# Gating of a conv MLP kept inside its up projection, with h tiles that take over the activations' memory kind by kind

## The chip, the cores and the metric

The kernel runs on one core of a Trainium2 chip. The metric is the time of one execution in microseconds (us). The engines are PE (TensorE, matrix products), DVE (VectorE), ACT (ScalarE), POOL (GpSimd) and SP (SyncE, which here only issues transfers).

## The reference

One layer on 656 columns (a prompt of 512 tokens with 16 meta tokens ahead, and 8 streams of 16). Its first half ends in an output projection (called "out" below) that is added to x. The change touches the second half:

```
up = rmsnorm(x) @ w_up              # 2048 -> 2 * 5632
g, v = up[..., :D_FF], up[..., D_FF:]
gext = concatenate([hist, g])       # two earlier rows of g
gc = conv_b + sum_k gext[k:k+seqlen] * conv_w[k]     # k = 0, 1, 2
h = gelu(gc) * v
y = x + h @ w_down                  # 5632 -> 2048, then a last rmsnorm
```

## The kernel before

Activations lie transposed: 128 channels on the partitions, 640 columns. The 5632 channels of g, v and h are 44 tiles, f = 0 to 43.

**Products.** Each fp32 operand is split into a high part (a cast by ACT) and a low part (a subtraction by DVE); a product is three matmuls, wh·xh, wh·xl and wl·xh. One helper issues all ACT, DVE and POOL operations, so the profile shows them under L130, and all matmuls stand under L157: operations are told apart by their tile names.

**Order.** The program is emitted once, with a modelled clock. Background work (evictions, splits, gating) are Python generators that `E.spawn` puts into a list and `E.tick` (L231) steps between matmuls. An engine runs its own instructions strictly in the order of emission and waits on semaphores, so a spawned step has a fixed place in each engine's queue.

**Weights.** `load_raw` (transfer at L197) loads four weight tiles at a time into one of four buffers `wraw`; ACT casts them to `wh` (four buffers), DVE subtracts to `wl`, and then the next load is issued. `wtile` (L250) runs the six matmuls of a weight tile; one such load thus feeds 24 matmuls.

**Out projection** (tiles n = 0 to 15, L1326 to L1352). Each n is evicted by `evict_x2` (L1232): DVE adds PSUM to x, the sum is stored as x3, squared by ACT and added to `ssq` by DVE. `mix` (L1207) then forms from two n's, pair j, the seven kinds of activations (B11, T1, B21, B22, T2, T3, T4) of a one-level Strassen scheme, and `split_mix` (L1223) writes their high and low parts: pairs 0 to 5 into `XT`, pairs 6 and 7 into `XH`, which is a view of `H[0]`, the operand of out, and so has to wait for out's last matmuls.

**Up projection** (L1461 on). For each f seven chains, one per kind, in two halves of K: 14 units of 12 matmuls, 168 per f. `Up` loads and combines weights. `evict_up` (L1432) makes g and v of f. For f < `NEARLY` = 11, `early` (L1418) runs `gate` (L1388: scale by rstd, conv, gelu, times v) and stores h to DRAM (`h_d`). For the other 33, `late` (L1424) stores g and v to DRAM (`g_d`, `v_d`).

**Down projection** (L1565). h of f is the operand k = f, kept as `hid` (high and low) in a ring of 21 places. The places and the accumulators `acc` lie over `XT` and `XH`, all in one pool that is opened after up. `load_h` (L1490) brings back the 11 stored h, `split_h` (L1518) splits them, then the 16 tiles x3 are loaded into `acc` (L1532), and `gates` (L1539) loads g and v of f = 11 to 43, gates and splits them during the down projection. The work runs in chunks of K, `DCH` = 11, 10, 10 and 9 k's by 16 n's; a chunk's places come free together when it ends:

```
for f in range(NEARLY, NFF):
    while f - RING > passed[0]:
        yield
```

The last four k's form a tail in two column halves, at the end of which y is normalised and stored.

Of the kernel before, what the change touches and what calls it, by code (L numbers as in the profile page):

```python
# [4 lines left out]
F32 = mybir.dt.float32  # L5
# [12 lines left out]
NEARLY = len(DCH[0])  # L18
RING = 21
# [255 lines left out]
def body(tc, A):  # L275
# [20 lines left out]
    H = [hp0.tile([128, 8, 2, NT], F32R, name="H0"), hp1.tile([128, 8, 2, NT], F32R, name="H1")]  # L296
# [20 lines left out]
    with tc.manual_schedule():  # L317
# [861 lines left out]
        cm_x, xp = E.open("x", waits="tile")  # L1179
# [75 lines left out]
        class Up:  # L1255
            def load(self, f, name, half):
                tag = "wraw" if (name == "A22") == (f > 0) and name != "A12" else "wr"
                self.put(f, name, half, tag)
                SP.dma_start(out=R[f, name, half], in_=A["wup"][(f * 4 + UP_LOADS.index(name)) * 2 + half])
# [8 lines left out]
            def start(self):  # L1268
                for name in ("A11", "A21"):
                    for half in range(2):  # L1270
                        self.load(0, name, half)

            def add(self, u):
# [5 lines left out]
                if p == "P1":  # L1279
                    self.put(f, "P1", h, "wraw" if f else "wr")  # L1280
# [45 lines left out]
        up = Up()  # L1326
        pss = [mm4() for _ in range(2)]
# [9 lines left out]
        for n in range(2, 16):  # L1337
            ps, t = mm4()
            for k in range(8):
                xh, xl = hsl(0, k, NC)  # L1340
                if n == 15 and k == 2:
                    up.start()
                if n == 15 and k in (4, 6):
                    up.split(k // 2 - 2)
# [5 lines left out]
            E.spawn(evict_x2(n, ps, t), 0, True)  # L1350
        while any(e in E.bg for e in E.bg):
# [12 lines left out]
        rps = [bank1(), bank1()]  # L1364
        rg = rstd_calc(ssq, rstd, 2 * XW, rps)
        next(rg)
        cm_f6.__exit__(None, None, None)
        cm_f7, f7 = E.open("f7", side="right", waits="tile")
        up.pool = f7
        for name in ("A22", "A12"):  # L1370
            for half in range(2):
                up.load(0, name, half)
            if name == "A22":
                up.add(2)
                up.add(3)

# [47 lines left out]
        def late(f, g, v):  # L1424
            yield from V.done()
# [343 lines left out]
```

## Time and profile before

| | |
|---|---|
| median of 3 runs | 2480.56 us (2479.4 to 2481.27) |
| profiled execution | 2479.52 us, its span 2477.7 us |
| mean granted clock of PE | 0.978 of full |
| busy: PE / DVE / ACT / POOL | 2359.6 / 1695.7 / 946.9 / 377.4 us |
| DRAM | 115 GB/s over the span |

The span runs from the first instruction to the last; all times below are on its scale. Out ends at 674.0, up at 1780.6 and the chunks of down at 2403.5. A busy share is an average over stages with different limits, so the views by stretch and the timelines say more than the page's first section.

### The profile page before, as it was taken

How to read it: one execution, taken by the hardware profiler on the slowest of the kernel's cores; microseconds unless marked ns; L12 is line 12 of the kernel's file. 1: busy time of each engine (PE TensorE's matmuls, PEld its weight loads, DVE VectorE, ACT ScalarE, POOL GpSimd, SP SyncE). 2: the span in 40 equal slices, each digit the busy share in tenths (PEclk: the TensorE clock that was granted, in tenths of full speed). 3: DMA queues.
4: the chain of work that ended last, by engine and by line, in shares of the span. 5: the costliest groups of instructions: out<-in, count | busy, mean ns of one | idle time of the engine just before them, and what ended most of it. 6: DMA issues, size and time to landing. Idle time of an engine off the chain costs nothing. (4 is left out here: it accounts for less than half of the span.)

```text
span 2477.7 us, 41060 instructions
## 1 busy us (share of the span) xinstructions
PE 2359.6 (95%) x15696; PEld 2340.1 (94%) x15696; DVE 1695.7 (68%) x2908; ACT 946.9 (38%) x1661; POOL 377.4 (15%) x596
## 2 busy tenths in 40 slices
PE   8998889999999999999999999999889999798997
PEld 7898889999999999999999999999889999798997
DVE  6489988446688888666666666666556666666636
ACT  5233444234444444333333333333323333333324
POOL 6746433000000000000000000000000000100004
PEclk9999999999999999999999999999989999899999
DMA  5332335534433333333333333333453334333323
GB/s 168 100 88 63 100 103 166 171 127 158 145 97 105 93 105 104 110 115 108 114 109 114 110 114 110 113 110 111 150 179 117 119 103 120 103 114 110 100 77 111
DMA packets 158343, 287.17 MB, mean 116 GB/s; under 512 B 22145, under 2 KB 42753, under 8 KB 158145
## 3 DMA queue, kind: packets, MB, share of 16 engines
q1 hardware_dynamic: 149024, 258.45, 34.6%
q0 software_dynamic: 8976, 26.08, 3.1%
q8 instruction: 123, 2.02, 0.3%
q14 instruction: 76, 0.61, 0.1%
q10 hardware_dynamic: 144, 0.01, 0.0%
HBM read 235.46 MB, written 49.00 MB: 115 GB/s over the span
## 5 line engine op out<-in xcount | busy, mean ns | idle before, releaser
L157 PE MATMUL pu<-XT,wh 128*128 128x320 f32 (+1 forms) x3696 | 827.0, 311 | 2.9 <-ACT wh L130 2.9
L157 PEld LDWEIGHTS pu<-XT,wh 128*128 128x128 f32 x3696 | 624.1, 189 | 3.8 <-ACT wh L130 3.4
L157 PE MATMUL pu<-XT,wl 128*128 128x320 f32 (+1 forms) x1848 | 573.2, 310 | 0.2 <-DVE wl L130 0.2
L130 DVE TENSOR_TENSOR wl<-wraw,wh 128x512 fp32r<-128x512 f32 (+1 forms) x487 | 342.7, 707 | 162.5 <-ACT wh L130 158.6
L130 DVE TENSOR_TENSOR wl<-wr,wh 128x512 fp32r<-128x512 f32 x438 | 302.5, 691 | 206.3 <-ACT wh L130 206.0
L130 ACT CAST wh<-wr 128x512 fp32r<-128x512 f32 x438 | 271.8, 621 | 441.9 <-PE pu L157 374.5
L130 ACT CAST wh<-wraw 128x512 fp32r<-128x512 f32 (+1 forms) x487 | 296.1, 614 | 291.9 <-PE pu L157 136.7
L157 PE MATMUL mm<-H,wh 128*128 128x320 f32 (+2 forms) x1920 | 383.0, 322 | 16.4 <-DVE H L130 8.8
L157 PEld LDWEIGHTS pu<-XT,wl 128*128 128x128 f32 x1848 | 350.2, 190 | 0.8 <-DVE wl L130 0.7
L157 PEld LDWEIGHTS mm<-H,wh 128*128 128x128 f32 x1920 | 310.0, 193 | 21.0 <-DVE H L130 8.7
L157 PE MATMUL md<-hid,wh 128*128 128x320 f32 x1280 | 245.6, 314 | 35.7 <-ACT hid L130 25.2
L157 PE MATMUL pu<-H,wh 128*128 128x320 f32 (+1 forms) x1232 | 276.8, 310 | 0.0
L157 PE MATMUL me<-hid,wh 128*128 128x320 f32 x1280 | 244.5, 314 | 0.0
L157 PEld LDWEIGHTS md<-hid,wh 128*128 128x128 f32 x1280 | 204.1, 191 | 39.0 <-ACT hid L130 26.7
L157 PE MATMUL mm<-H,wl 128*128 128x320 f32 x960 | 225.9, 317 | 5.7 <-DVE wl L130 5.7
L157 PEld LDWEIGHTS pu<-H,wh 128*128 128x128 f32 x1232 | 206.4, 188 | 0.0
L157 PEld LDWEIGHTS me<-hid,wh 128*128 128x128 f32 x1280 | 205.6, 192 | 0.0
L157 PE MATMUL pu<-H,wl 128*128 128x320 f32 (+1 forms) x616 | 191.1, 310 | 0.0
L157 PEld LDWEIGHTS mm<-H,wl 128*128 128x128 f32 x960 | 166.5, 193 | 7.1 <-DVE wl L130 7.1
L157 PE MATMUL md<-hid,wl 128*128 128x320 f32 x640 | 148.0, 313 | 8.9 <-DVE wl L130 8.9
L157 PE MATMUL me<-hid,wl 128*128 128x320 f32 x640 | 147.9, 313 | 0.0
L130 ACT ACTIVATE f<-f 128x640 f32<-128x640 f32 (+2 forms) x91 | 66.8, 734 | 171.9 <-DVE f L130 169.9
(223 smaller groups left out, 2791.9 us busy)
## 6 DMA issues: line engine op xcount, KB each, us to landing
wraw<-wts SPq DMA_DIRECT2D x323, 256.0 KB, 2.7
wr<-wup SPq DMA_DIRECT2D x262, 256.0 KB, 2.7
wraw<-wup SPq DMA_DIRECT2D x90, 256.0 KB, 2.7
g_d<-f POOLq DMA_DIRECT2D x33, 322.0 KB, 2.8
f<-g_d SPq DMA_DIRECT2D x33, 322.0 KB, 3.2
v_d<-f POOLq DMA_DIRECT2D x33, 320.0 KB, 2.5
f<-v_d SPq DMA_DIRECT2D x33, 320.0 KB, 3.9
w<-yg_d SPq DMA_DIRECT2D x16, 328.0 KB, 3.3
```

What stands on the lines that cost most here:

```text
L130: return f(*a, **k)
L157: return self.eng.matmul(out=out, lhsT=lhsT, rhs=rhs, start=start, stop=stop, **more)
```

## The change

- All 44 f are gated inside up and stored as `h_d`; `g_d`, `v_d`, `late` and `gates` are gone.
- The ring has 23 places of two sorts. `hida`, eight, lie over `H[0]` and `XH`; `hidb`, 15, lie over `XT` with `acc`, and are opened once gating has ended.
- `XH` is now seven tiles, one per kind, over `H[0]`, each as large as an h place: a `hida` place comes free when the last up chain of its kind has been run.
- An h is loaded straight into its place and split there. `feed` loads two h ahead, and once the `hidb` places are open it loads x3 four at a time between them.
- Where out meets up: the first weights of up are loaded earlier, A22 into places of x2 and A21 a second time into `xa`; `ssq` lies in `rstd`; the eviction of n = 15 and the last pair's odd kinds run as a background step in the first units of up (PE waits for a kind that isn't `ready`); `rstd_calc` runs from unit 10 on.

The number of matmuls is the same. Core of the diff:

```diff
-NEARLY = len(DCH[0])
-RING = 21
+RING0, RING1 = 8, 15
+RING = RING0 + RING1
...
-    H = [hp0.tile([128, 8, 2, NT], F32R, name="H0"), hp1.tile([128, 8, 2, NT], F32R, name="H1")]
+    H = [[hp0.tile([128, 2, NT], F32R, name=f"H0_{k}") for k in range(8)], hp1.tile([128, 8, 2, NT], F32R, name="H1")]
...
-    g_d = {f: dp.tile([128, 2, XW], F32, name=f"g_d{f}") for f in range(NEARLY, NFF)}
-    v_d = {f: dp.tile([128, 640], F32, name=f"v_d{f}") for f in range(NEARLY, NFF)}
-    h_d = [dp.tile([128, 640], F32, name=f"h_d{f}") for f in range(NEARLY)]
+    h_d = [dp.tile([128, 640], F32, name=f"h_d{f}") for f in range(NFF)]
...
-        cm_x, xp = E.open("x", waits="tile")
+        cm_x, xp = E.open("x", side="right", waits="tile")
...
-        XH = H[0].rearrange("p k h c -> p (k h c)")[:, 0:2 * 2 * 7 * XW].rearrange("p (k h t c) -> p k h t c", k=2, h=2, t=7)
-
-        def xpair(j, h):
-            return XT[:, j, h] if j < KP - 2 else XH[:, j - (KP - 2), h]
+        XH = {}
+
+        def xkind(j, h, ty):
+            return XT[:, j, h, ty] if j < KP - 2 else XH[ty][:, j - (KP - 2), h]
...
-        ssq = f6.tile([128, 2 * XW], F32, name="ssq2")
+        ssq = rstd[:, 0:2 * XW]
+
+        def x2tile():
+            return f6.tile([128, 2, XW], F32, tag="x2", name="x2", bufs=4)
 
         def load_x2p(n):
-            x2[n] = f6.tile([128, 2, XW], F32, tag="x2", name="x2", bufs=3)
+            x2[n] = x2tile()
...
-            S.copy(out=xpair(j, 0)[:, lo:hi], in_=tb[:, lo:hi])
-            yield from S.done()
-            TT(xpair(j, 1)[:, lo:hi], tb[:, lo:hi], xpair(j, 0)[:, lo:hi].bitcast(F32), SUB)
+            if j < KP - 2:
+                kinds = [slice(B21, T4 + 1) if odd else slice(B11, T1 + 1)]
+                dst = lambda h, k: XT[:, j, h, k]
+            else:
+                kinds = [T4, T3, T2, B21, B22] if odd else [B11, T1]
+                dst = lambda h, k: XH[k][:, j - (KP - 2), h]
+            for k in kinds:
+                S.copy(out=dst(0, k), in_=tb[:, k])
+            yield from S.done()
+            for k in kinds:
+                TT(dst(1, k), tb[:, k], dst(0, k).bitcast(F32), SUB)
+                if j >= KP - 2:
+                    ready.add((j, k))
...
+            def start_a22(self):
+                for half in range(2):
+                    R[0, "A22", half] = x2tile().rearrange("p a c -> p (a c)")[:, 0:CH * 128].rearrange("p (c m) -> p c m", c=CH)
+                    self.fetch(0, "A22", half)
+
+            def again_a21(self):
+                for half in range(2):
+                    R[0, "A21", half] = xa.tile([128, CH, 128], F32, tag="xa", name="xa", bufs=2)
+                    self.fetch(0, "A21", half)
...
+                if (n, k) in ((14, 6), (15, 2)):
+                    for half in range(2):
+                        up.load(0, "A11" if n == 14 else "A21", half)
                 if n == 15 and k == 2:
-                    up.start()
-                if n == 15 and k in (4, 6):
-                    up.split(k // 2 - 2)
+                    up.start_a22()
+                if n == 15 and k in (4, 5):
+                    up.split(k - 4)
+                if n == 15 and k == 6:
+                    up.add(2)
+                    up.add(3)
+                if n == 15 and k == 7:
+                    up.split(2)
...
+            if n < 15:
+                E.spawn(evict_x2(n, ps, t), 0, True)
+        while E.bg:
             E.tick(True)
+        cm_h0.__exit__(None, None, None)
+        cm_xh, xhp = E.open("xh", waits="tile")
+        for ty in (B11, T1, T4, T3, T2, B21, B22):
+            XH[ty] = xhp.tile([128, 2, 2, XW], F32R, name=f"XH{ty}")
+        cm_xa, xa = E.open("xa", waits="tile")
+        up.again_a21()
         for j in range(KP - 2, KP):
             E.drain(split_mix(j, 0))
-        for j in range(KP - 2, KP):
-            E.drain(split_mix(j, 1))
+        E.drain(split_mix(KP - 2, 1))
+        up.split(3)
+
+        def last_x2(ps, t):
+            yield from evict_x2(15, ps, t)
+            yield from split_mix(KP - 1, 1)
+
+        gen = last_x2(ps, t)
+        next(gen)
+        E.spawn(gen, 1)
...
-        def late(f, g, v):
-            yield from V.done()
-            nc.gpsimd.dma_start(out=v_d[f], in_=v[:, 0:640])
-            nc.gpsimd.dma_start(out=g_d[f], in_=g)
...
-                E.spawn((early if f < NEARLY else late)(f, g, T_["v"]))
+                E.spawn(early(f, g, T_["v"]))
...
+            if u == 6:
+                while E.bg:
+                    E.tick(True)
+                cm_xa.__exit__(None, None, None)
+                cm_f6.__exit__(None, None, None)
+                cm_f7, f7 = E.open("f7", side="right", waits="tile")
+                up.pool = fpool[0] = f7
+                for half in range(2):
+                    up.load(0, "A12", half)
+                for l in up.later:
+                    up.load(*l)
+                E.drain(evict_up(0, 0))
+            if u == 10:
+                E.spawn(rstd_calc(ssq, rstd, 2 * XW, [bank1(), bank1()]))
...
+            if f == 0 and h and ty != B11:
+                while (KP - 1, ty) not in ready:
+                    E.tick(True)
...
+        cm_xh.__exit__(None, None, None)
+        cm_l0, lp0 = E.open("lp0", waits="tile")
...
+        def hidtile():
+            i = nhid[0] % RING
+            nhid[0] += 1
+            if i < RING0:
+                return lps[0].tile([128, 2, 2 * XW], F32R, tag="hida", name="hida", bufs=RING0)
+            return lps[1].tile([128, 2, 2 * XW], F32R, tag="hidb", name="hidb", bufs=RING1)
...
+            hraw[f] = hidtile()
+            SP.dma_start(out=hraw[f][:, 1, 0:640].bitcast(F32), in_=h_d[f])
+
+        def split_h(f):
+            t = hraw.pop(f)
+            hi, lo = t[:, 0, 0:640], t[:, 1, 0:640]
+            S.copy(out=hi, in_=lo.bitcast(F32))
+            yield from S.done()
+            TT(lo, lo.bitcast(F32), hi.bitcast(F32), SUB)
+            hid[f] = t
...
+        for f in range(5):
+            load_h(f)
+        for f in range(3):
+            E.drain(split_h(f))
+        while (NFF - 1, 6) not in evicted:
...
-        for f in range(NEARLY):
-            if f == 3:
-                acc = lp.tile([128, 16, 640], F32, name="acc")
-            E.drain(split_h(f, he.pop(f)))
-            if f + 3 < NEARLY:
-                load_h(f + 3)
-        for n in range(16):
-            SP.dma_start(out=half2(acc[:, n]), in_=x3_d[n])
...
-        def gates():
-            ld = {}
-
-            def load(f):
-                g, v = f26().rearrange("p (a c) -> p a c", a=2), f26()
-                SP.dma_start(out=g, in_=g_d[f])
-                SP.dma_start(out=v[:, 0:640], in_=v_d[f])
-                ld[f] = g, v
-
-            load(NEARLY)
-            yield 4
-            for f in range(NEARLY, NFF):
-                while f - RING > passed[0]:
-                    yield
-                g, v = ld.pop(f)
-                if f + 1 < NFF:
-                    load(f + 1)
-                yield from gate(f, g, v, 2)
-                yield from split_h(f, v)
...
+        def feed():
+            for f in range(3, NFF):
+                if f + 2 == RING0:
+                    while gating[0]:
+                        yield
+                    cm_f7.__exit__(None, None, None)
+                    cm_x.__exit__(None, None, None)
+                    cm_l1, lps[1] = E.open("lp1", waits="tile")
+                    cm_f8, fpool[0] = E.open("f8", side="right", waits="tile")
+                    fpool[1] = 8
+                    D.update(cms=(cm_l1, cm_f8), acc=lps[1].tile([128, 16, 640], F32, name="acc"),
+                             ssq=fpool[0].tile([128, 640], F32, name="ssq3"))
+                    for g in range(4):
+                        SP.dma_start(out=half2(D["acc"][:, g]), in_=x3_d[g])
+                    x3n = 4
+                if f + 2 < NFF:
+                    while f + 2 - RING > passed[0]:
+                        yield
+                    load_h(f + 2)
+                if f + 2 > RING0 and x3n < 16:
+                    for g in range(x3n, x3n + 4):
+                        SP.dma_start(out=half2(D["acc"][:, g]), in_=x3_d[g])
+                    x3n += 4
+                yield from split_h(f)
+                yield from V.done()
+
+        E.spawn(feed())
```

Three places in the engines' orders (names in front of `<-` are what is written).

**DVE where out ends.** `x` is the eviction of out's last tile, n = 15 (`x_7151` before, `x_7124` now); `H_77` and `XH` are the low parts of pairs 6 and 7; `tb` the kinds in fp32. Before:

```order
L130 TENSOR_TENSOR wl<-wraw,wh 128x512
L130 TENSOR_TENSOR tb<-tb 128x322
L130 TENSOR_TENSOR wl<-wraw,wh 128x512
L130 TENSOR_TENSOR ssq_6071<-ssq_6071,q 128x644
L130 TENSOR_TENSOR x_7151<-mm,x_7151 128x2x320
L130 TENSOR_TENSOR x_7151<-mm,x_7151 128x2
L130 SCALAR_TENSOR_TENSOR tb<-tb 128x322
L130 TENSOR_TENSOR tb<-tb 128x322 x2
L130 TENSOR_TENSOR ssq_6071<-ssq_6071,q 128x644
L130 TENSOR_TENSOR H_77<-tb,H_77 128x644 x2
```

Now:

```order
L130 TENSOR_TENSOR wl<-wraw,wh 128x512
L130 TENSOR_TENSOR XH_7227<-tb,XH_7227 128x322
L130 TENSOR_TENSOR XH_7228<-tb,XH_7228 128x322
L130 TENSOR_TENSOR XH_7227<-tb,XH_7227 128x322
L130 TENSOR_TENSOR XH_7228<-tb,XH_7228 128x322
L130 TENSOR_TENSOR XH_7229<-tb,XH_7229 128x322
L130 TENSOR_TENSOR XH_7230<-tb,XH_7230 128x322
L130 TENSOR_TENSOR XH_7231<-tb,XH_7231 128x322
L130 TENSOR_TENSOR XH_7232<-tb,XH_7232 128x322
L130 TENSOR_TENSOR XH_7233<-tb,XH_7233 128x322
L130 TENSOR_TENSOR wl<-wraw,wh 128x512
L130 TENSOR_TENSOR x_7124<-mm,x_7124 128x2x320
```

Before, the eviction of n = 15 stands ahead of the low parts of the last two pairs; now nine low parts and a weight tile stand ahead of it.

**ACT where down begins.** `hid` and `hida` casts are the splits of h; `wh` those of weights; `gx` and `f` belong to gating. Before (the last of eleven `hid` casts in a row, and what follows):

```order
L130 CAST hid<-f_19388 128x640
L130 CAST hid<-f_19393 128x640
L130 CAST wh<-wraw 128x512 x2
L130 COPY gx<-gx 128x2x31
L130 ACTIVATE f_19496<-gx,vec 128x640
L130 CAST wh<-wraw 128x512
L130 ACTIVATE f_19497<-f_19496 128x640
L130 CAST wh<-wraw 128x512
L130 ACTIVATE f_19497<-f_19497 128x640
```

Now, from the first weight cast of down on:

```order
L130 CAST wh<-wraw 128x512
L130 CAST hida<-hida 128x640 x3
L130 COPY gx<-gx 128x2x31
L130 ACTIVATE f_19883<-gx,vec 128x640
L130 CAST wh<-wraw 128x512
L130 CAST hida<-hida 128x640
L130 CAST wh<-wraw 128x512
L130 ACTIVATE f_19884<-f_19883 128x640
L130 CAST hida<-hida 128x640
L130 CAST wh<-wraw 128x512
```

Before, eleven h splits stood ahead of the second weight cast; now three, and the gating of f = 43 stands between the splits.

**SP there.** Before, five weight loads, eleven loads of h and sixteen of x3 stand in a row; its beginning:

```order
L1259 DMA wr<-wup 128x512 x6
L197 DMA wraw<-wts 128x512 x5
L1492 DMA f_19339<-h_d_201 128x640
L1492 DMA f_19341<-h_d_202 128x640
L1492 DMA f_19343<-h_d_203 128x640
```

Now, from the fifth of the first run of h loads on (`hida` is the place, `h_d` the source):

```order
L1557 DMA hida<-h_d_146 128x640
L1557 DMA hida<-h_d_147 128x640
L197 DMA wraw<-wts 128x512 x2
L1557 DMA hida<-h_d_148 128x640
L197 DMA wraw<-wts 128x512
L1557 DMA hida<-h_d_149 128x640
L197 DMA wraw<-wts 128x512
L1598 DMA acc<-x_d_126 128x640
L1598 DMA acc<-x_d_127 128x640
L1598 DMA acc<-x_d_128 128x640
L1598 DMA acc<-x_d_129 128x640
L1557 DMA hidb<-h_d_150 128x640
```

The h and x3 loads now alternate with weight loads, and the first `hidb` load stands behind four loads of x3.

## Rows read from the trace of the kernel before

**Rows 1.** Waits of PE over the span: us in total, times, longest us.

```profile
PE md L157 <- ACT hid L130: 25.2, 5, 6.9
...
PE pu L157 <- DVE ssq L130: 4.7, 1, 4.7
```

**Rows 2.** Chain of waits: start us, us, engine and tile; last chunk boundary, and the tail.

```profile
2280.11 0.73 ACT hid L130
...
2292.58 7.92 PE md L157 x54
...
2403.46 0.54 PE md L157 x3
```

**Rows 3.** Stretch: length, busy PE, PEld, DVE, ACT, POOL, clock, DMA share, GB/s.

```profile
674.03:740.77 66.74, 58.97 (x370) 57.07 (x370) 54.20 (x89) 33.78 (x54) 3.82 (x7) 0.95 0.31 90
715.91:964.45 248.54, 248.54 (x1682) 248.54 (x1682) 216.74 (x351) 116.67 (x202) 20.38 (x40) 1.00 0.35 99
989.28:1759.73 770.45, 770.45 (x5211) 770.45 (x5210) 517.18 (x837) 289.82 (x497) 37.02 (x93) 1.00 0.37 112
1780.55:2403.46 622.91, 578.25 (x3841) 575.05 (x3842) 369.53 (x532) 202.68 (x340) 48.38 (x67) 0.96 0.38 119
1965.00:1985.00 20.00, 16.43 (x100) 15.94 (x99) 13.59 (x20) 8.44 (x14) 2.90 (x4) 0.91 0.40 134
2110.00:2145.00 35.00, 21.07 (x122) 19.72 (x122) 23.52 (x34) 12.89 (x21) 4.35 (x6) 0.76 0.32 96
2270.00:2295.00 25.00, 18.21 (x108) 17.60 (x107) 16.98 (x25) 9.14 (x16) 2.91 (x4) 0.86 0.34 105
```

**Rows 4.** PE's timeline, down begins: start us, us, instruction [idle before <-releaser].

```profile
1780.24 0.31 PE L157 MATMUL pu<-H,wl 128*128 128x320 f32 x1
1782.59 0.41 PE L157 MATMUL md<-hid,wh 128*128 128x320 f32 x1 [2.04 <-ACT hid L130]
...
1797.58 1.44 PE L157 MATMUL md<-hid,wh 128*128 128x320 f32 x4 [8.96 <-ACT wh L130]
...
1812.54 0.90 PE L157 MATMUL md<-hid,wl 128*128 128x320 f32 x2 [8.92 <-DVE wl L130]
```

**Rows 5.** PE's timeline where out ends and up begins, columns as in rows 4.

```profile
678.73 2.49 PE L157 MATMUL pu<-ssq,ones 128*128 128x320 f32 x4 [4.69 <-DVE ssq L130]
```

**Rows 6.** ACT's timeline where down begins.

```profile
1781.81 0.72 ACT L130 CAST hid<-f 128x640 fp32r<-128x640 f32 x1 [6.04 <-DMA f<-h_d]
...
1785.89 1.50 ACT L130 CAST hid<-f 128x640 fp32r<-128x640 f32 x2 [1.01 <-DMA f<-h_d]
...
1812.21 0.92 ACT L130 ACTIVATE f<-gx,vec 128x640 f32<-128x640 f32 x1
1813.04 0.60 ACT L130 CAST wh<-wraw 128x512 fp32r<-128x512 f32 x1
```

**Rows 7.** SP's queue where down begins: start us, us, line, transfer.

```profile
1778.85 13.51 SPq L1492 DMA_DIRECT2D f<-h_d  x11
1792.41 11.36 SPq L1532 DMA_DIRECT2D acc<-x_d  x16
```

**Rows 8.** DVE's timeline where out ends.

```profile
670.26 0.69 DVE L130 TENSOR_TENSOR wl<-wraw,wh 128x512 fp32r<-128x512 f32 x1 [2.37 <-ACT wh L130]
670.87 0.49 DVE L130 TENSOR_TENSOR tb<-tb 128x322 f32<-128x322 f32 x1
...
671.88 0.82 DVE L130 TENSOR_TENSOR ssq<-ssq,q 128x644 f32<-128x644 f32 x1
674.07 0.89 DVE L130 TENSOR_TENSOR x<-mm,x 128x640 f32<-128x640 f32 x2 [1.37 <-PE mm L157]
```

**Rows 9.** Transfers: tile, queue, times, KB each, median us from issue to landing.

```profile
h_d<-f POOLq DMA_DIRECT2D x11, 320.0 KB, 2.5
```

**Rows 10.** Stretches of the hand-over, columns as in rows 3.

```profile
1795.00:1800.00 5.00, 2.42 (x9) 2.43 (x10) 2.85 (x4) 2.33 (x4) 0.00 (x0) 0.50 0.91 314
1800.00:1805.00 5.00, 3.62 (x21) 3.36 (x19) 0.00 (x0) 0.00 (x0) 0.00 (x0) 0.87 1.04 406
```

More of the change, by code (lines that the diff above doesn't have):

```diff
@@ L1258, in load, with fetch @@
                 self.put(f, name, half, tag)
+                self.fetch(f, name, half)
+            def fetch(self, f, name, half):
                 SP.dma_start(out=R[f, name, half], in_=A["wup"][(f * 4 + UP_LOADS.index(name)) * 2 + half])
@@ L1279, in add @@
                 if p == "P1":
-                    self.put(f, "P1", h, "wraw" if f else "wr")
+                    if f:
+                        self.put(f, "P1", h, "wraw")
+                    else:
+                        R[f, "P1", h] = r("A21")
                     TT(r("P1"), r("A21"), r("A22"), ADD)
@@ L1300, in free @@
                 if f + 1 < NFF:
-                    self.load(f + 1, name, h)
+                    if self.pool is None:
+                        self.later.append((f + 1, name, h))
+                    else:
+                        self.load(f + 1, name, h)
             def hi(self, u):
@@ L1326, in body @@
         up = Up()
+        up.pool, up.later = None, []
         pss = [mm4() for _ in range(2)]
@@ L1362, in bank1 @@
             return pu.tile([128, 512], F32, tag="pu", name="pu", bufs=8)
[L1364 to L1375, printed above, removed]
         def f26():
             return fpool[0].tile([128, 2 * XW], F32, tag="f26", name="f26", bufs=fpool[1])
-        fpool = [f7, 5]
+        fpool = [None, 5]
         w26 = f26
-        E.spawn(rg)
         gating = [0]
@@ L1455, in evict_up @@
                 TT(g[:, 1, 0:320], e[:, 0:320], T_["u2"], ADD)
-                E.spawn((early if f < NEARLY else late)(f, g, T_["v"]))
+                E.spawn(early(f, g, T_["v"]))
+            evicted.add((f, c))
             yield
-        up.split(2)
         mm = T.matmul
+        PB[0, 4] = bank1()
         for u, (f, c, h) in enumerate(UN):
@@ L1483, in body @@
                 E.tick()
-            if h:
-                E.spawn(evict_up(f, c), 0, True)
-        he = {}
-        def load_h(f):
-            he[f] = f26()
-            SP.dma_start(out=he[f][:, 0:640], in_=h_d[f])
-        for _ in range(8):
-            E.tick(True)
-        for f in range(3):
-            load_h(f)
-        while E.bg:
-            E.tick(True)
-        cm_x.__exit__(None, None, None)
-        cm_h0.__exit__(None, None, None)
+            if h and u > 1:
+                E.spawn(evict_up(f, c), 2 if u == len(UN) - 1 else 0, True)
+        cm_xh.__exit__(None, None, None)
+        cm_l0, lp0 = E.open("lp0", waits="tile")
+        lps = [lp0, None]
+        nhid = [0]
+        hid, hraw = {}, {}
+        def hidtile():
[4 more added lines that the diff above has]
+            return lps[1].tile([128, 2, 2 * XW], F32R, tag="hidb", name="hidb", bufs=RING1)
+        E.keep = hidtile
+        def load_h(f):
+            hraw[f] = hidtile()
[12 more added lines that the diff above has]
+        while (NFF - 1, 6) not in evicted:
+            E.tick(True)
         cm_pu.__exit__(None, None, None)
         cm_pd, pd = E.open("pd", bufs=2, space=PSUM, waits="tile")
-        cm_l, lp = E.open("lp", waits="tile")
-        hid = {}
-        def hidtile():
-            return lp.tile([128, 2, 640], F32R, tag="hid", name="hid", bufs=RING)
-        E.keep = hidtile
         def mm4():
@@ L1516, in mm4 @@
             return [t[:, 0, :], t[:, 1, :]], t
-        def split_h(f, v):
-            h = hidtile()
-            S.copy(out=h[:, 0], in_=v[:, 0:640])
-            yield from S.done()
-            TT(h[:, 1], v[:, 0:640], h[:, 0].bitcast(F32), SUB)
-            hid[f] = h
-        for f in range(NEARLY):
-            if f == 3:
-                acc = lp.tile([128, 16, 640], F32, name="acc")
-            E.drain(split_h(f, he.pop(f)))
-            if f + 3 < NEARLY:
-                load_h(f + 3)
@@ L1559, in body @@
-        E.spawn(gates())
+        passed = [-1]
+        D = {}
+        def feed():
[23 more added lines that the diff above has]
+                yield from V.done()
@@ L1586, in body @@
             passed[0] = ks[-1]
+        acc, ssq = D["acc"], D["ssq"]
         def fin_acc(n, o, w, p, last):
```

30 lines of the change are left out of this document (12 added, 18 removed).

## The prediction, made before the changed kernel had run

> **What bounds the kernel now.** I read first what PE waits for, then the chain of waits for the price of a matmul, then the busy time by stretch, and last the timelines where PE stands still. PE's waits name two families: five waits of 25.2 us in all for a cast of h (`hid`), and 4.7 us for `ssq` where out ends [rows 1]. The chain ends at such a wait (a `hid` cast at 2280.11) and is from there on matmuls alone, 54 in 7.92 us, which is 0.1467 us each [rows 2]. By that price each stretch shows what it loses. In up PE is busy for 100% of the time at full clock, in the stretch where f is gated (715.91 to 964.45, ten f) as in the one where it isn't (989.28 to 1759.73, 31 f) [rows 3]; there a faster engine gains nothing. The losses lie elsewhere:
>
> - Down. Up ends at 1780.24 + 0.31 = 1780.55 [rows 4], the tail begins at 2403.46 [rows 2]. The chunks are 40 k by 16 n by 6 = 3840 matmuls, 563.2 us; they take 622.9, so 59.7 are lost. In the three stretches around the chunk boundaries there are 100, 122 and 108 matmuls in 20, 35 and 25 us [rows 3]: 5.3 + 17.1 + 9.2 = 31.6 lost. The other 28.1 are lost where up hands over to down: PE stands still for 2.04, 8.96 and 8.92 us [rows 4], the rest is smaller stops and half clock after them.
> - Out to up. From 674.03 to 740.77 there are 370 matmuls [rows 3], 54.3 us of 66.7: 12.4 lost, of them 4.69 in one wait [rows 5].
>
> **The change part by part.**
>
> *1. Boundaries: 31.6 to 0.* Before, h of a chunk is gated in the down projection and needs a place that comes free only when a chunk ends; the `hid` cast is the last link of that gating. Now an h costs one load, one cast of 0.72 [rows 6] and one subtraction of about that size. With 23 places, h of k = 11 to 20 needs no chunk to end, and k = 23 to 33 only the first. In the order of emission they are split by weight tile 70 and 218, and used from tile 176 and 336: over 100 tiles of 0.88 us ahead. The cover is so thick that I take the whole 31.6; the other bound is 0, if PE still waits there.
>
> *2. Up to down: 28.1 to 5.2.* The first stop stays. The first h load stands on SP behind the fifth weight load as before, issued at 1778.85 [rows 7]; its cast could start at 1781.81 [rows 6]. That kind-0 places are free much earlier isn't used. Counting the stop and the half clock after it, k = 0 ends at 1797.58 − 8.96 = 1788.62 [rows 4], 8.07 after up's end; its 24 matmuls take 3.52, so 4.55 are kept. The 8.96 and 8.92 go: ACT had eleven `hid` casts ahead of the second weight cast, and DVE's next `wl` stood behind a gating step whose g was loaded after sixteen x3, 11.36 us of SP [rows 7]. Now three casts of h (0.72), a small copy, one activation (0.92) and the cast of weights (0.60) [rows 6] stand there. If the third h lands as late as before (cast at 1785.89 [rows 6]), the weights are cast at 1785.89 + 0.72 + 0.92 + 0.60 = 1788.1; without the store of g in its way I estimate 1786.3. PE wants them at 1788.62: hidden, with 0.5 to 2.3 us to spare. What is late next is the burst of x3 (rival 1), which I charge 0.7, about a fifth of a weight load's 3.52. Bounds of this part: 4.5 and 12.
>
> *3. Out to up: 12.4 to 8.5.* Before, PE finished n = 15 at 678.73 − 4.69 = 674.04 [rows 5], DVE evicted it at 674.07 [rows 8], and PE waited for `ssq`, the norm being first in up. Now rstd comes later, but on DVE more stands ahead of that eviction, and the first up matmuls need it too, as they take over its PSUM. From 670.26, by starts of following rows (a `wl` 0.61, a `tb` 0.40) [rows 8]: two `wl` 1.22, `tb` 0.40, two weight sums 1.22, `ssq` 0.82, `wl` 0.61, nine low parts of 322 columns 3.6, `wl` 0.61, the eviction 0.89: 9.4, so until 679.6. PE stops for about 5.6, 0.9 more than the 4.69 before, and then runs matmuls of up at once. For half clock I take 2.0, since the first stop of down cost 4.55 − 2.04 = 2.5 with it and a smaller stop [rows 4], and 0.9 for waits on the last pair's kinds: 8.5, a gain of 3.9. Bounds of the gain: 1 (three us more of half clock or waits) and 5.
>
> *4. Gating of 33 more f inside up: 0.* Gated, DVE is busy 216.74 / 10 = 21.67 us per f, ungated 517.18 / 31 = 16.68; an f lasts 24.85 in both [rows 3]. So 5.0 us per f lie beside PE with 3.2 to spare. ACT has 11.7 of 24.85. Uncovered it would cost 33 × 5.0 = 165. The same gating leaves down, where DVE wasn't the bound but for part 1.
>
> *5. DRAM.* g, v and their transfers fall away, h rises from 11 to 44 tiles. Up's transfers take 0.35 to 0.37 of the engines' time [rows 3]: 0.
>
> Sum: 2479.5 − 31.6 − (28.1 − 5.2) − 3.9 = 2421.1. The profiled execution stands 1.0 below the median of the runs, so I take 2421.5.
>
> **The rivals.**
>
> *1. The burst of x3 starves the weights.* Four x3 go out once the last gated h is stored, which I put at 16 us after up's end (gating, then 2.5 for the store [rows 9]), and then alternate with h and weights. Until weight load 12 that is 16 × 0.328 + 5 × 0.328 + 4 × 0.262 = 7.9 MB. PE wants its matmuls at 4.5 + 12 × 3.52 = 46.8 after up's end, less 3.5 for the load ahead and 2 for landing and cast: 41.3. The transfers start about 2 us after the issue, at 18.2, so 7.93 MB in 23.1 us, 343 GB/s, decide. The stretches of the hand-over show 406 GB/s, and 314 where other work runs [rows 10]. At 406 there are 3.6 us to spare, at 314 a stop of 2.2 with 1.6 of half clock, and two or three such stops are possible, as loads 9 to 11 also stand behind x3: 2425 to 2433. Against: x3 comes four at a time. The Trainium skill, page "DMA: Bandwidth & Descriptors", section "Where 436 GB/s comes from", puts the limit of a core's memory side at about 358 GB/s, which would leave 1 us to spare; the trace's 406 is above it, so the measurement decides.
>
> *2. The second weight cast is late.* If the three h land later than before, because they now share the transfers with loads of weights, the 0.5 to spare above is used up and a second stop of 1 to 3 us with half clock comes: 2424 to 2427. For it: three casts still stand ahead. Against: no g is stored or loaded at that moment.
>
> *3. The boundary waits stay,* in that a chunk waits for something else that is freed late: 2421.5 + 31 = 2452. Against: over 100 tiles of cover.
>
> *4. Slower: DVE becomes the bound of up.* The change gates 33 f more while weight sums and subtractions have to keep pace. It outweighs the 58.4 gained when over 58.4 / 33 = 1.8 us per f show up; all 5.0 give 2479.5 − 58.4 + 165 = 2586. For it: DVE at 87% in that stretch [rows 3] has little room, and PE waits for the end of v's gating before it starts a chain. Against: ten f already ran so without a lost microsecond.
>
> **How the numbers follow.** Forecast 0.64 (2413 to 2427); rival 1 0.16; rival 2 0.08; rival 3 0.04; rival 4 0.04; about the same time, if new stops eat the gain, 0.04. Its low end takes parts 2 and 3 at their best bounds (4.5 and 5) and, as a further possibility, the first stop of down shortened by the places that come free early, some 5 us; so 2413. The high end takes rival 1 fully and part 3 at its worst: 2436. What a measurement of this kernel can tell from no change is about 0.2%, 5 us. Faster 0.92 (forecast, rivals 1 to 3), same 0.03, slower 0.05 (rival 4 and a quarter of the last case).
>
> **What would show it.** PE's waits for `hid` no longer at 1965, 2130 and 2280 but one of about 2 us after up; no stop of 9 us behind it; 24.85 us per f up to f = 43 with DVE at 21 to 22 us in each; a stop of 5 to 6 us where out ends, ended by the eviction of n = 15. Chunks of down in about 568 us. Wrong would be: PE below 100% in up, waits for weights 15 to 45 us after up's end, or PE waiting at a chunk's start.

## The result, and the profile after

The changed kernel takes 2419.91 us (median of 4 runs, 2418.75 to 2421.22), the one before 2479.98 (4 runs, 2478.44 to 2481.27) on the same chips: a ratio of 0.9758, 95% interval 0.9741 to 0.9775. The forecast was 2421.5, range 2413 to 2436. The profiled execution has a span of 2417.5 us against 2477.7, 60.2 less.

PE's waits, where [rows 1] stood before. No wait for `hid` at a boundary is left, and none for weights in down:

```profile
PE pu L157 <- DVE x L130: 5.4, 1, 5.4
...
PE md L157 <- ACT hida L130: 1.9, 1, 1.9
PE pu L157 <- DVE f L130: 1.5, 1, 1.5
...
PE md L157 <- DVE hida L130: 0.4, 1, 0.4
...
PE md L157 <- DVE acc L130: 0.2, 1, 0.2
```

The busy time by stretch, columns as in [rows 3]: out to up, up in two pieces (both gated now), the chunks of down, and in it the three stretches in which a chunk ends (its 1056th, 2016th and 2976th matmul, at 1934.7, 2075.4 and 2216.0):

```profile
673.57:738.10 64.53, 57.59 (x369) 56.55 (x370) 52.40 (x97) 32.72 (x60) 3.81 (x7) 0.95 0.31 93
738.10:961.24 223.14, 223.14 (x1514) 223.14 (x1513) 194.96 (x316) 104.93 (x182) 18.29 (x36) 1.00 0.34 100
986.03:1754.62 768.59, 768.59 (x5210) 768.59 (x5209) 671.43 (x1086) 361.60 (x621) 63.10 (x124) 1.00 0.34 100
1775.35:2342.63 567.28, 564.75 (x3842) 564.29 (x3841) 186.73 (x276) 132.82 (x212) 1.29 (x2) 1.00 0.34 110
1930.00:1955.00 25.00, 25.00 (x173) 25.00 (x172) 10.81 (x16) 8.96 (x14) 0.00 (x0) 1.00 0.42 137
2070.00:2105.00 35.00, 35.00 (x241) 35.00 (x240) 15.43 (x23) 13.02 (x20) 0.00 (x0) 1.00 0.46 157
2210.00:2240.00 30.00, 30.00 (x207) 30.00 (x206) 6.72 (x11) 4.96 (x8) 0.00 (x0) 1.00 0.26 78
```

What to see: in the third row 31 f are gated, DVE does 671.43 / 31 = 21.66 us per f (16.68 before), and PE is still busy all the time at full clock. The fourth row has PE idle for 2.5 us in all of down's chunks, nearly all of it at their start; the last three have no stop where a chunk ends. DVE's work in down has halved (186.73, 369.53 before).

Where the 60.2 us came from, stretch by stretch (out's end, an early f's `m` eviction at 738.10, up's end and the tail's first matmul, from the timelines; down from [rows 2] and the same row of the chain of waits after, `2342.79 0.53 PE md L157 x3`):

| stretch | before | after | difference | forecast |
|---|---|---|---|---|
| start to out's end | 674.03 | 673.57 | −0.5 | 0 |
| out to up | 66.74 | 64.53 | −2.2 | −3.9 |
| rest of up, 41 f and its end | 1039.78 | 1037.25 | −2.5 | 0 |
| chunks of down | 622.91 | 567.44 | −55.5 | −54.5 |
| tail | 74.2 | 74.7 | +0.5 | 0 |

### The profile page after: what moved, and what is told of

It reads as the page before. It is cut to its first block, busy times and chain, and to the rows that moved or that the text cites. A ratio compares the mean times of both kernels' runs of the same rounds, so it can differ in the third digit from the quotient of the medians.

```text
span 2417.5 us, 41020 instructions
## 1 busy us (share of the span) xinstructions
PE 2339.6 (97%) x15696; PEld 2323.8 (96%) x15696; DVE 1672.8 (69%) x2918; ACT 951.1 (39%) x1671; POOL 356.4 (15%) x563
## 4 chain that ended last, share of the span: by engine, by line
PE 74%; DVE 2%; issue 1%; DMA 1%; ACT 0%; SPq 0%; DVEq 0%; POOL 0%; ACTq 0%; POOLq 0%
PE pu L157 44%; PE me L157 12%; PE md L157 12%; PE mm L157 4%; PE mf L157 2%; DVE acc L130 1%; DMA acc<-x_d 1%; DVE f L130 0%; DVE wl L130 0%; DMA hidb<-h_d 0%; DVE XH L130 0%; DMA h_d<-f 0%; DVE wr L130 0%; ACT f L130 0%; ACT wh L130 0%
## 5 line engine op out<-in xcount | busy, mean ns | idle before, releaser
L157 PE MATMUL pu<-XT,wh 128*128 128x320 f32 (+1 forms) x3696 | 825.3, 311 | 6.9 <-DVE x L130 5.4
L157 PEld LDWEIGHTS pu<-XT,wh 128*128 128x128 f32 x3696 | 621.7, 189 | 7.5 <-issue 5.6
L157 PE MATMUL pu<-XT,wl 128*128 128x320 f32 (+1 forms) x1848 | 572.8, 310 | 0.0
L157 PE MATMUL mm<-H,wh 128*128 128x320 f32 (+2 forms) x1920 | 380.7, 320 | 15.3 <-DVE H L130 7.3
L157 PEld LDWEIGHTS pu<-XT,wl 128*128 128x128 f32 x1848 | 349.9, 189 | 0.2 <-DVE wl L130 0.2
L157 PEld LDWEIGHTS mm<-H,wh 128*128 128x128 f32 x1920 | 308.4, 192 | 19.7 <-ACT H L130 7.9
L157 PE MATMUL pu<-XH,wh 128*128 128x320 f32 (+1 forms) x1232 | 277.3, 310 | 0.0
L157 PE MATMUL mm<-H,wl 128*128 128x320 f32 x960 | 225.4, 316 | 5.6 <-DVE wl L130 5.5
L157 PEld LDWEIGHTS pu<-XH,wh 128*128 128x128 f32 x1232 | 207.1, 189 | 0.3 <-DVE XH L130 0.3
L157 PE MATMUL pu<-XH,wl 128*128 128x320 f32 (+1 forms) x616 | 190.3, 309 | 0.0
L157 PEld LDWEIGHTS mm<-H,wl 128*128 128x128 f32 x960 | 165.6, 192 | 6.8 <-DVE wl L130 6.8
L130 DVE TENSOR_TENSOR acc<-me,acc 128x640 f32<-128x640 f32 (+2 forms) x48 | 34.0, 710 | 190.5 <-PE me L157 190.5
L130 DVE TENSOR_TENSOR acc<-md,acc 128x640 f32<-128x640 f32 (+2 forms) x48 | 34.1, 711 | 186.0 <-PE md L157 185.9
L157 PE MATMUL me<-hidb,wh 128*128 128x320 f32 x768 | 143.6, 309 | 0.0
L157 PE MATMUL md<-hidb,wh 128*128 128x320 f32 x768 | 143.6, 309 | 0.0
L157 PEld LDWEIGHTS me<-hidb,wh 128*128 128x128 f32 x768 | 120.8, 188 | 0.0
L157 PEld LDWEIGHTS md<-hidb,wh 128*128 128x128 f32 x768 | 120.8, 188 | 0.0
L130 DVE TENSOR_TENSOR wr<-wr 128x512 f32<-128x512 f32 x172 | 118.4, 688 | 3.0
```

The lines of the kernel that those rows point to most:

```text
L130: return f(*a, **k)
L157: return self.eng.matmul(out=out, lhsT=lhsT, rhs=rhs, start=start, stop=stop, **more)
```

## The experiments

Ten kernels ran. The profiled executions are compared by two stretches, since the time up to out's end, which no edit but those of out's last tile touches, lies between 671.1 and 675.6 us from execution to execution. Each group was timed beside the kernel before, whose median was 2478.95 to 2479.98 us each time, so that the medians may be set side by side.

| kernel | median us | out's end to up's end | up's end to tail |
|---|---|---|---|
| before | 2479.98 | 1106.5 | 622.7 |
| changed | 2419.91 | 1101.8 | 567.3 |
| e1 gating alone | 2441.36 | 1106.7 | 585.3 |
| e2 eviction first | 2412.4 | 1095.8 | 567.4 |
| e3 h first | 2419.63 | 1102.3 | 567.3 |
| e4 = e2 + e3 | 2413.78 | 1095.9 | 569.5 |
| e5 = e4, x3 singly | 2412.4 | 1095.9 | 566.3 |
| e6 = e5, h 0 split early | 2410.71 | 1095.9 | 564.4 |
| e7 x3 in one burst | 2427.69 | 1102.3 | 574.4 |
| e8 DVE + 2 | 2426.6 | 1103.7 | 571.5 |
| e9 DVE + 5 | 2608.66 | 1288.3 | 567.9 |
| e10 XT shifted | 2421.92 | 1102.0 | 566.9 |

**e1: the gating alone**, put into the kernel before.

```diff
+NUP = 43
-                E.spawn((early if f < NEARLY else late)(f, g, T_["v"]))
+                E.spawn((early if f < NUP else late)(f, g, T_["v"]))
...
+                if f < NUP:
+                    g, v = None, f26()
+                    SP.dma_start(out=v[:, 0:640], in_=h_d[f])
+                    ld[f] = g, v
+                    return
...
-                yield from gate(f, g, v, 2)
+                if f >= NUP:
+                    yield from gate(f, g, v, 2)
                 yield from split_h(f, v)
+                yield from V.done()
```

> The kernel before, with one part of the change alone: f = 11 to 42 are gated inside up too and their h is loaded and split in the down projection (f = 43 stays as before, gated in down); ring of 21, old hand-over, old out-to-up. Theory: the 31.6 us at the chunk boundaries came from gating in down, so they vanish with this part alone, and of the hand-over's 28.1 the last stop of 8.92 with its half clock shrinks to at most a few us because only one tile is gated there: 2435 to 2449 us, up at 24.85 us per f as before, the stop of 9.0 behind the eleven casts still there. Rival: the boundary stops came from the ring's size and its freeing by chunks, which stay as they were; then PE still waits for hid at the boundaries and the time stays above 2465. Second question, the 24.79 us per f of the changed kernel: if it comes from gating all f in up, it shows here; if from where the activations lie, up stays at 24.85 here.

Measured: 2441.36 us (2440.72 to 2444.45, 5 runs), ratio 0.9849 (0.9836 to 0.9862). PE's waits (lines are one higher there), and the stretches of up's middle and of down from 60 us behind its start:

```profile
PE md L158 <- ACT wh L131: 14.0, 2, 8.1
...
PE md L158 <- ACT hid L131: 2.2, 1, 2.2
```

```profile
900.00:1700.00 800.00, 800.00 (x5411) 800.00 (x5409) 696.48 (x1127) 375.22 (x644) 65.13 (x128) 1.00 0.34 100
...
1840.00:2364.00 524.00, 524.00 (x3574) 524.00 (x3574) 161.80 (x241) 110.38 (x178) 0.73 (x1) 1.00 0.28 90
```

The five waits for `hid` are one; behind 1840 PE never stops, with the old ring of 21 places and its freeing by chunks. So the boundary stops came from gating in down, and the rival falls. The hand-over still loses 22.1 (585.3 − 563.2): the 8.07 behind eleven casts, and 5.93, where at most a few us were expected, for a weight cast behind the next `hid` cast, whose load stood behind sixteen x3:

```profile
1789.55 11.14 SPq L1533 DMA_DIRECT2D acc<-x_d  x16
...
1801.20 0.32 SPq L1546 DMA_DIRECT2D f<-h_d  x1
...
1807.84 0.72 ACT L131 CAST hid<-f 128x640 fp32r<-128x640 f32 x1 [13.29 <-DMA f<-h_d]
```

The other 18 us of the gain in down (585.3 − 567.3) thus belong to the new hand-over as a whole, but for some 0.6 of pace (see the part on the prediction). e7 puts the x3 back in one run; three casts in place of eleven weren't tried alone.

**e2: the eviction of out's last tile ahead of the low parts.**

```diff
         while E.bg:
             E.tick(True)
+        def last_x2(ps, t):
+            yield from evict_x2(15, ps, t)
+            yield from split_mix(KP - 1, 1)
+
+        gen = last_x2(ps, t)
+        next(gen)
         cm_h0.__exit__(None, None, None)
...
-        gen = last_x2(ps, t)
-        next(gen)
         E.spawn(gen, 1)
```

> The changed kernel, with the eviction of out's last tile moved on DVE ahead of the nine low parts of the last pairs. Theory: PE's stop of 5.38 us where up begins is only the place of that eviction in DVE's queue; moved, it can run within about 1.5 us of out's end, and the first up matmuls read pairs 0 to 5, whose parts are long there: a stop of 1 to 2 us, less half clock, 4 to 6 us faster: 2414 to 2416. Rival: DVE's total work there (9 us of it between 669.5 and 678.8) is the limit, and PE meets the same delay in small pieces at pairs 6 and 7 and at the weights of the next units: within 1.5 us of the changed kernel.

Measured: 2412.4 us (2410.55 to 2415.05, 5 runs), ratio 0.9733 (0.972 to 0.9745) against 0.9758 for the changed kernel. First DVE and PE of the changed kernel where out ends, then DVE and PE of e2:

```profile
673.68 3.72 DVE L130 TENSOR_TENSOR XH<-tb,XH 128x322 fp32r<-128x322 f32 x9
677.32 0.68 DVE L130 TENSOR_TENSOR wl<-wraw,wh 128x512 fp32r<-128x512 f32 x1
677.92 0.88 DVE L130 TENSOR_TENSOR x<-mm,x 128x640 f32<-128x640 f32 x2
```

```profile
678.95 0.88 PE L157 MATMUL pu<-XT,wh 128*128 128x322 f32 x2 [5.38 <-DVE x L130]
```

```profile
672.29 0.89 DVE L130 TENSOR_TENSOR x<-mm,x 128x640 f32<-128x640 f32 x2
673.09 3.72 DVE L130 TENSOR_TENSOR XH<-tb,XH 128x322 fp32r<-128x322 f32 x9
```

```profile
673.32 0.55 PE L157 MATMUL pu<-XT,wh 128*128 128x322 f32 x2 [1.14 <-ACT XH L130]
```

And the busy time behind the two stops, first the changed kernel, then e2:

```profile
678.95:683.10 4.15, 4.15 (x15) 4.15 (x16) 0.13 (x1) 0.62 (x1) 0.00 (x0) 0.50 0.22 79
```

```profile
673.30:677.00 3.70, 3.68 (x25) 3.70 (x26) 3.70 (x10) 3.49 (x8) 0.00 (x0) 1.00 0.67 225
```

The same work of DVE in another order: the stop is 1.14 in place of 5.38, the half clock behind it is gone, and the stretch up to up's end is 6.0 us shorter. (The last row of the timeline names a step of ACT; the eviction ends 0.14 us before PE starts, 0.15 in the changed kernel.) DVE's sum was not the limit. The time is 1.6 us below the expected 2414: the gain in the stretch lies at the upper end of the 4 to 6 expected, and out's end, which the profiled execution reaches 1.4 us earlier, varies by more than that.

**e3: three h loads ahead of the fifth weight load.**

```diff
-                E.split_lo()
+                E.split_lo(False)
...
         for f in range(5):
             load_h(f)
+            if f == 2:
+                E.load_raw()
```

> The changed kernel, with the first three h loads issued on SP ahead of the fifth weight load of the down projection, the other weight loads as they were. Theory: the 4.1 us that down still loses come from the first h load standing behind that weight load, which waits for a buffer; issued earlier, the h places of the first kinds being free, the h are cast before up ends and the stop of 1.86 us, the 0.44 after it and the half clock go: 3 to 4.5 us faster, 2415.5 to 2417. Rival: the first casts stand on ACT behind the last weight casts of up, and the PSUM of the first down tile is free only after up's last eviction, so that a stop of about 1.5 us remains whatever SP does: less than 2 us gained.

Measured: 2419.63 us (2416.09 to 2421.39, 5 runs), ratio 0.9758: no gain. The rival's size holds (less than 2 us), but neither story has the cause. PE's stops in e3:

```profile
1776.97 0.70 PE L157 MATMUL md<-hida,wh 128*128 128x320 f32 x3 [2.10 <-DVE hida L130]
1818.07 0.83 PE L157 MATMUL md<-hida,wh 128*128 128x320 f32 x4 [2.28 <-DVE acc L130]
```

The wait for ACT is gone, but the low part of h 0 stands on DVE behind up's last eviction, so a stop of 2.10 stays; and what PE gained by then (2.0 us) it lost again at 1818 to the first `acc` additions.

**e4: both.**

> Both edits together, the eviction first and the first three h loads first. Theory: the two stops lie 1100 us apart, so the gains add: 7 to 10 us faster than the changed kernel, 2410 to 2413. Rival: one of the two doesn't gain, and the sum is the other alone.

Measured: 2413.78 us (2410.84 to 2416.4, 5 runs). The rival holds: e2's gain alone, and 2.30 lost at the `acc` additions. In e4 DVE stands as follows there:

```profile
1811.29 0.82 DVE L130 TENSOR_TENSOR hidb<-hidb 128x640 fp32r<-128x640 f32 x1 [3.25 <-ACT hidb L130]
1812.04 0.69 DVE L130 TENSOR_TENSOR wl<-wraw,wh 128x512 fp32r<-128x512 f32 x1
1812.64 0.82 DVE L130 TENSOR_TENSOR acc<-md,acc 128x640 f32<-128x640 f32 x1
```

The additions wait behind the split of an h whose load hasn't landed (ACT's cast of it waits 3.42 us for the transfer until 1810.53), in the stretch in which x3 and h fill the transfers. The changed kernel's rows of it (columns as in [rows 3]):

```profile
1800.00:1805.00 5.00, 5.00 (x36) 5.00 (x35) 2.85 (x4) 1.88 (x4) 0.00 (x0) 1.00 1.04 405
1805.00:1810.00 5.00, 5.00 (x36) 5.00 (x35) 1.43 (x2) 1.25 (x2) 0.00 (x0) 1.00 1.04 394
1810.00:1815.00 5.00, 5.00 (x36) 5.00 (x35) 1.43 (x2) 1.25 (x2) 0.00 (x0) 1.00 1.04 391
```

There the burst just fits: PE waits 0.23 us for `acc`. Two us earlier, it doesn't.

**e5: e4, with x3 one at a time after the first four.**

```diff
-                    for g in range(x3n, x3n + 4):
-                        SP.dma_start(out=half2(D["acc"][:, g]), in_=x3_d[g])
-                    x3n += 4
+                    SP.dma_start(out=half2(D["acc"][:, x3n]), in_=x3_d[x3n])
+                    x3n += 1
```

> The kernel of e4 with x3 loaded one tile at a time after the first four, in place of four at a time; the bytes are the same, but 8 of the 16 x3 loads (2.6 MB) move behind the h and weight loads that PE needs first. Theory: e3 gained nothing because PE, 2 us earlier, ran into the full DMA stretch after up (394 to 405 GB/s in the changed kernel): a split of h on DVE waits for its load, and the first four acc additions stand behind it. With 2.6 MB less ahead (6.5 us at 400 GB/s) that wait of 2.30 us and its half clock go: down loses 2.2 instead of 6.3 us against its full rate, so some 4 us under e4: 2408.5 to 2411. Rival: the wait hangs on DVE's order or on the acc tiles themselves, not on the bytes; then 2.3 us stay and the time is e4's, 2413 to 2415.

Measured: 2412.4 us (2412.03 to 2413.02, 5 runs). The 2.30 us at `acc` are gone, as expected, but the time falls short of 2411: down still loses 3.1, since behind the same stop of 2.10 at its start the clock now fell to half, which it hadn't in e4 (last section): 1.5 us, which the expectation hadn't counted.

**e6: h 0 and h 1 split on DVE ahead of up's last eviction.**

```diff
-        for f in range(3):
-            E.drain(split_h(f))
+        for f in range(2):
+            t = hraw.pop(f)
+            S.copy(out=t[:, 0, 0:640], in_=t[:, 1, 0:640].bitcast(F32))
+            TT(t[:, 1, 0:640], t[:, 1, 0:640].bitcast(F32), t[:, 0, 0:640].bitcast(F32), SUB)
+            hid[f] = t
+        E.drain(split_h(2))
```

> The kernel of e5 with the low parts of the first two h put on DVE ahead of the last eviction of up. Theory: in e3 and e4 the stop of 2.10 us at the first down matmuls is no longer the load but DVE's order, the low part of h 0 standing behind that eviction and two gating steps; moved, PE goes from up to down without a stop of over 0.5 us: 2 us under e5, 2406.5 to 2409. Rival: the load of h 0 or PSUM still ends later than up; then the stop stays.

Measured: 2410.71 us (2408.14 to 2412.07, 4 runs), ratio 0.9723 (0.971 to 0.9736). PE goes into down without a stop, and then waits twice for the second weights:

```profile
1771.17 0.85 PE L157 MATMUL md<-hida,wh 128*128 128x320 f32 x4 [0.66 <-ACT wh L130]
1772.85 0.56 PE L157 MATMUL md<-hida,wl 128*128 128x320 f32 x2 [0.83 <-DVE wl L130]
```

Down loses 1.2 in all, 2.9 less than in the changed kernel. The stop went as expected; the median is 1.7 us above the expected range, which had been counted from e5's. This is the fastest version, clear of the changed kernel by its interval, not of e2 (0.972 to 0.9745), e4 and e5.

**e7: all sixteen x3 in a row ahead of h 8.**

```diff
-                    for g in range(4):
+                    for g in range(16):
...
-                    x3n = 4
+                    x3n = 16
```

> The changed kernel with all sixteen x3 loads issued in a row, ahead of h 8 (rival 1 of the prediction made as bad as it can be). By the prediction's price: 5.2 MB at 395 GB/s are 13.3 us, h 8 lands some 10 us later than before and PE wants it about 32 us after the first x3 is issued, 16 us after it at the latest with splits: stops of 2 to 6 us between 1805 and 1820, more with half clock: 2422 to 2430. If the transfers were hidden with room to spare, the time stays within 1.5 us of the changed kernel.

Measured: 2427.69 us (2427.21 to 2428.53, 4 runs), as priced: one stop and half clock, 7.8 us over the changed kernel.

```profile
1811.05 1.44 PE L157 MATMUL md<-hida,wh 128*128 128x320 f32 x4 [5.92 <-ACT wh L130]
```

**e8 and e9: two and five more DVE operations per f** (one line twice, five times, behind the second conv step; results unused).

```diff
             STT(gcv, gf[:, 0:640], vcol(V_CW, f), gcv, MUL, ADD)
+            TT(sqv, gcv, gcv, MUL)
+            TT(sqv, gcv, gcv, MUL)
```

> The changed kernel with two extra DVE multiplications of 128 x 640 per f in the gating, whose result is overwritten (rival 4 made worse on purpose): some 1.5 us more DVE work per f, 23.2 of 24.8. Theory: still hidden beside PE, up stays at 24.8 us per f, and only the gating of f = 43 at the hand-over gets longer: 2419 to 2423. Rival: the queue of DVE is already the limit, because its order and not its sum counts; then 44 times up to 1.5 us show: up to 2485.

> As e8 with five extra DVE multiplications per f: 3.7 us more, 25.4 us of DVE work in a stretch of 24.8. e8 left up at 24.79 us per f, so its 6.7 us more came from both ends of up. Theory (rival 4 decides where DVE's sum passes PE's): up now goes at DVE's pace, 25.3 to 25.7 us per f, 20 to 40 us over 44 f, and both ends of up lose some 10 more: 2445 to 2475. If up slows by much more than the excess of DVE's sum, its order in the queue counts as well; if it stays at 24.8, the estimate of DVE's sum is off.

Measured: e8 2426.6 us (2424.39 to 2431.09, 4 runs), e9 2608.66 (2606.56 to 2609.75, 4 runs). The same 800 us of up in e8 and in e9, then PE's waits in e9:

```profile
900.00:1700.00 800.00, 800.00 (x5423) 800.00 (x5422) 737.70 (x1196) 374.30 (x646) 66.57 (x131) 1.00 0.33 100
```

```profile
900.00:1700.00 800.00, 715.77 (x4608) 702.12 (x4607) 700.83 (x1100) 313.28 (x551) 57.36 (x111) 0.97 0.28 86
```

```profile
PE pu L157 <- DVE f L130: 92.5, 42, 3.3
PE pu L157 <- DVE wl L130: 39.5, 43, 3.0
```

A busy time of 737.70 us over 5423 / 168 = 32.3 f is 22.9 per f, so that e8 adds 1.2 us to the 21.66 of the changed kernel, not the 1.5 estimated. With these up's pace doesn't move: 1.2 of slack are shown. What e8 loses is at the ends: 1.9 more in up, and in down a wait of 4.09 for `acc`, because f = 43's longer gating delays its store, behind which x3 is issued (19.9 us after up's end, 16.3 in the changed kernel). The total is 3.6 over the expected range.

In e9 the same sum is 25.6 (4608 / 168 = 27.4 f), 3.9 more than in the changed kernel. Up loses (1288.3 − 1101.8) / 44 = 4.2 us per f, five times the 0.8 by which DVE's sum passes 24.8, and DVE is busy for only 88% of the time. So expectation and measure part: the sum alone doesn't give the loss. The two waits above, for evictions (`f`) and for `wl`, are 132 us or 3.0 per f; part of the rest is half clock (0.97 in the 800 us). So these steps come up late in DVE's queue; how much of that is order and how much the sum isn't separated. The five extra operations stand in one block of 4.3 us, and the edit moves other steps too, as the modelled clock that places them moves with it. In e9 the eviction that reads `m` comes ahead of `u`, soon behind the last gating steps; in the changed kernel and in e8 it comes behind `u` and two more evictions:

```profile
1227.10 1.68 DVE L130 SCALAR_TENSOR_TENSOR f<-f,f 128x640 f32<-128x640 f32 x2
...
1229.29 0.49 DVE L130 TENSOR_TENSOR f<-pu,m 128x322 f32<-128x322 f32 x1
1229.70 0.48 DVE L130 TENSOR_TENSOR u<-pu,u 128x320 f32<-128x320 f32 x1
```

Rival 4 was to decide from 1.8 us per f that show in up: e8 shows none, e9 4.2, so the cliff lies between 1.2 and 3.9 us more work than the change gives DVE, for work put at this place.

**e10: XT moved by 64 bytes.**

```diff
+        xp.tile([128, 16], F32, name="pad")
         XT = xp.tile([128, KP - 2, 2, 7, XW], F32R, name="XT")
```

> The changed kernel with XT moved by 64 bytes on every partition (an unused tile stands ahead of it). It asks where the 24.79 us per f come from, against 24.85 in the kernel before, which e1 kept with all gating but one in up. If the address of the moving operands sets the small extra time of a matmul, the pace of up changes from 24.79 to another value (24.7 to 24.9, so 2415 to 2425); if the pace stays at 24.79, the position of XT to within 64 bytes has no part in it, and the time is that of the changed kernel, 2418.5 to 2421.5.

Measured: 2421.92 us (2418.86 to 2425.63, 4 runs), 24.79 us per f: a shift of 64 bytes has no part in the pace.

## Why the prediction was right

*Part 1* (boundaries, 31.6 to 0): as forecast. The stretches in which chunks end show 100% for PE (rival 3 fell), and e1 shows that gating in down was the reason for the stops.

*Part 2* (hand-over, 28.1 to 5.2): 4.2 are left (567.44 − 563.2); at the changed kernel's own price of 0.1465 us per matmul 4.9 are lost. The first stop is the one kept, 1.86 and 0.44 us, with half clock. The second weights were cast at 1780.84, 5.5 us after up's end, where 5.8 (1786.3) had been estimated, and no stop stands there: rival 2 fell. The first x3 was issued 16.3 us after up's end (forecast 16):

```profile
1780.24 0.60 ACT L130 CAST wh<-wraw 128x512 fp32r<-128x512 f32 x1
```

```profile
1791.64 1.75 SPq L1598 DMA_DIRECT2D acc<-x_d  x4
```

Rival 1 was close by: the transfers ran at 391 to 405 GB/s against a decision at 343, and e3 and e4 show that two us less leave a stop (2.28 and 2.30 us), e7 that one burst costs 7.1 us in down. The stop came not at a weight load, as priced, but at the first additions, which DVE's order puts behind an h. The Trainium skill's limit of about 358 GB/s ("DMA: Bandwidth & Descriptors", "Where 436 GB/s comes from") didn't bind here: 405 was measured.

*Part 3* (out to up, gain 3.9): half of it came, 2.2. The stop was 5.38 where 5.6 had been summed; the eviction began 677.92 − 673.57 = 4.4 us after out's end, where 679.6 − 0.9 − 674.0 = 4.7 had been put. The 0.9 for waits on the last pair's kinds didn't show up in PE's waits; a wait of 1.54 for DVE at 730.23 that wasn't in the sum did:

```profile
730.23 0.53 PE L157 MATMUL pu<-XT,wh 128*128 128x320 f32 x2 [1.54 <-DVE f L130]
```

The last steps of f = 0's gating stand in DVE's queue ahead of the eviction that PE needs, with one `wl` between (1.68 us from 726.88). They are late because rstd, moved from ahead of up into its first f, is formed on DVE just before: this gating began 5.8 us behind the last matmul of its f, that of the following f 1.7. The half clock behind the first stop cost 2.0 as taken (15 matmuls in 4.15 us, shown at e2). The term was mis-sized by the wait at 730.23 and within its bounds (1 to 5); its 12.4 at the outset is 12.0 at up's own price of 24.85 / 168 = 0.148 us per matmul, where down's had been used. What the prediction didn't ask is whether the order that it summed had to be so; e2 shows it needn't.

*Part 4* (gating at no cost): as forecast, no loss in up, and e8 shows slack left. *Part 5* (DRAM): no difference seen.

What was not foreseen is 2.5 us in up's pace: 24.79 us per f in place of 24.85. e1 has 24.85 with all gating but one in up, so that this isn't the gating, nor the stores that went away; e8's extra DVE work and e10's shift leave it at 24.79. Down has it too: 500 us hold 3415 matmuls here (those cut at both ends included), 0.1465 us each from start to start, where e1's row of 1840.00:2364.00 gives 0.1467; over 3840 matmuls that is some 0.6 of down's 55.5.

```profile
1840.00:2340.00 500.00, 500.00 (x3415) 500.00 (x3414) 151.05 (x225) 104.83 (x168) 0.00 (x0) 1.00 0.29 90
```

What sets it stays open. Moving the whole XT from one end of the memory to the other, as the change does, wasn't tried.

Forecast and result differ by 1.6 us; with the two misses of +1.7 and −2.5, and 1.0 less lost in down, the agreement is a little better than its terms: part of it is luck. Two small sums of the prediction don't come out: the low end's terms give 2414.7 (2421.5 − 0.7 − 1.1 − 5), not 2413, and the 1.0 between the profiled execution and the median would make 2422.1 of 2421.1, not 2421.5. Neither decides anything here.

## What to carry to other kernels

Price a stop together with what stands in front of it in the queue that ends it: two pieces here (18 us where up meets down, 6 us behind nine subtractions) were work in the wrong order, not too much work. For the second e2 shows it by an edit of the order alone; for the first it is read from the traces, as the change altered order and work together. Work can be moved into a stretch in which another engine is the bound as long as its latest result still comes in time in that engine's queue; the sum of busy time alone doesn't say so (in e9 DVE is busy for 88%, and 4.2 us per f are lost). A stop that is removed lets the next one show, which is why e3 gained nothing until e5 and e6 had taken away the next two.

## What the runs showed of the hardware

The same stop isn't always followed by half clock. The stop of 2.10 us at the start of down had none behind it in e3 and e4, but did in e5, which has e4's code at that place. The granted clock from the stop's end to 1776 shows it (1.00 and 0.54), first e4, then e5:

```profile
1771.88:1776.00 4.12, 4.12 (x28) 4.09 (x29) 3.91 (x6) 3.36 (x6) 0.16 (x1) 1.00 0.88 313
```

```profile
1772.28:1776.00 3.72, 3.72 (x15) 3.72 (x16) 3.35 (x5) 2.20 (x4) 0.17 (x1) 0.54 0.90 290
```

In 3.72 us at full clock there is room for 25 matmuls of 0.147, and e5 ran 15: 10 × 0.147 = 1.5 us hang on the moment at which a stop falls, more than some edits here are worth. The Trainium skill ("TensorE: Matmul & The Clock Gate", "Part 1: The HAM clock gate (the "warmup" mystery)") says that the window by which the clock is gated runs freely, so that one kernel shows different numbers of slow matmuls from run to run. The five runs of e3 fit this, with mean granted clocks of 0.987 to 0.991 and times of 2416.09 to 2421.39 us; only one of them was profiled, so that where they differ isn't shown.
